# Keys and queries stored with the high and low part of a feature side by side, so that a head's tile is loaded on all 128 partitions

## The chip, the cores and the metric

One core of one Trainium2 chip runs the whole program. The metric is device time in microseconds (us). The kernel before took 2184.16 us, the median of three runs (2183.7 to 2186.5).

The core has TensorE (PE in the profile, with PEld for its weight loads), VectorE (DVE), ScalarE (ACT), GpSimd (POOL) and SyncE (SP). In this kernel nearly all DMA transfers are issued from SP's queue, in the order in which they stand there, and are carried out by 16 DMA engines that the profile shows as one busy share.

## The reference

One layer of a streaming encoder on 1024 positions of 1024 features, all in float32:

```
x = x + 0.5 * swiglu_ffn(rms_norm(x), ffn1)
u = rms_norm(x);  q_a k_a v_a q_b k_b v_b gate = split(u @ w_mix_in)
y_a = softmax(q_a k_a^T / 8 + rel_bias, band of 9 chunks of 64) v_a        # 8 heads of 64
p1, p2 = softmax(q_b[r] k_b[r]^T / 8 + t5_bias, chunk-causal)  r = 0, 1    # 4 heads, 2 x 64 features
y_b = rms_norm((p1 - lam * p2) v_b) * (1 - lambda_init)
x = x + (sig(g_a) * (y_a @ w_branch_a) + sig(g_b) * (y_b @ w_branch_b)) @ w_o
x = x + 0.5 * swiglu_ffn(rms_norm(x), ffn2);   out = rms_norm(x)
```

What matters here is the score product q k^T: 64 features per head, 1024 keys.

## The kernel before

**Split operands.** Large products are done three times: an operand is split into a part `hi`, which ScalarE rounds to float32r, and the rest `lo` (VectorE, source minus `hi`), and a product a·b becomes hi·hi + hi·lo + lo·hi (`mm3`, L128 to L130). The feed-forward and projection products are moreover done with a Strassen scheme of seven products on half matrices.

**The stages.** First feed-forward block (up to about 690 us of the profiled execution), the mixer's input projection (to about 1075 us), attention (1075 to about 1385 us), the output projection of the mixer, the second feed-forward block.

**Projection.** For each of eight index values n, `Pair` produces 128 features of the queries and 128 of the keys (n = 0 to 3: two heads of branch A each; n = 4 to 7: one head of branch B, whose two halves r are 64 features each), on [128 features, 512 positions] pieces. `qk_sink(n)` splits such a piece and writes `hi` and `lo` by `move` (L124) to the DRAM tensors `q_d[n]` and `k_d[n]`. Their shape is [2, 128, 1024]: all `hi` rows, then all `lo` rows. A piece is 256 KB, and a key piece costs two stores. The split pieces `qkh` lie in a ring of ten buffers (tag "f") that other pieces of the projection share.

**Attention.** For each n, `load_qkv(n)` brings three tiles of [128, 2, 1024] into SBUF (the middle index is the head, or r): `qs` holds `hi` of the 64 query features on partitions 0 to 63 and `lo` on 64 to 127; `ks` holds `hi` of the keys twice, `kl` holds `lo` twice. One matmul against `ks` (L775) and one against `kl` (L776) over 128 partitions then add up the four products. Since one DMA fills one half of the partitions, each n needs six DMAs of 512 KB ([64, 2, 1024]), then `vt` (values, 1 MB) and, for the A pairs and every second B head, eight DMAs of the bias `nb`.

The work of one n is a list of jobs (`jobs_a`: 8, `jobs_b`: 8 with growing width). `run` keeps up to four jobs in flight, a stage apart: scores and softmax (L775, L776, L783, L785), transposes `pt` (L791), the product with the values `pv` (L860 for A, L939 and L940 for B), and for B the output transpose `try` (L954). Between B's jobs `branch_a` puts pieces of the next projection, `pb` (12 matmuls each, L128 to L130), which load a gate piece `gl` and store the result (`ta`, L889).

**What sets the order.** The order of each engine's instructions is set when the program is built, by a scheduler that plays a model of the timeline; each engine then goes through its own list strictly in order and waits at an instruction whose operands are not there. SP does the same: an issue waits until its tile's buffer is free, and until the eighth DMA before it in the queue has landed (eight completion counters are used in turn). The tiles `qs`, `ks`, `kl`, `vt`, `y` and `nb` share a ring of 14 buffers (tag "big"), so that the loads of the next n are issued while the present one is worked on.

Of the kernel before, what the change touches and what calls it, by code (L numbers as in the profile page):

```python
# [10 lines left out]
F32R = mybir.dt.float32r  # L11
# [5 lines left out]
P = 128  # L17
S = 1024
# [3 lines left out]
HALF = 512  # L22
# [32 lines left out]
def hybrid_layer_kernel(ctx, tc, x, ffn1_norm, ffn1_w_in, ffn1_w_out, mix_norm, w_mix_in,  # L55
# [3 lines left out]
    nc = tc.nc  # L59
# [9 lines left out]
    def big(shape, name, dtype=F32R):  # L69
        return sb.tile(shape, dtype, tag="big", bufs=14, name=name)  # L70
# [7 lines left out]
    def temp(shape, name="temp"):  # L78
        return sb.tile(shape, F32, tag="f", bufs=TF, name=name)
# [14 lines left out]
    def split(src, hi, lo, scale=None, on_pool=False):  # L94

        if scale is None:
            nc.scalar.copy(out=hi, in_=src)  # L97
        else:
            nc.scalar.activation(out=hi, in_=src, func=AF.Copy, scale=scale)
        h = hi.bitcast(F32)  # L100
        if scale is None:
            (nc.gpsimd if on_pool else nc.vector).tensor_tensor(out=lo, in0=src, in1=h, op=ALU.subtract)  # L102
        else:
            nc.vector.scalar_tensor_tensor(out=lo, in0=src, scalar=scale, in1=h,
                                           op0=ALU.mult, op1=ALU.subtract)
# [16 lines left out]
    def move(eng, dst, src):  # L122

        eng.dma_start(out=dst.bitcast(F32), in_=src.bitcast(F32))  # L124
# [394 lines left out]
    def drams(n, shape, name, dtype=F32):  # L519
        return [dram.tile(shape, dtype, name=f"{name}{i}") for i in range(n)]  # L520
# [44 lines left out]
    x_part = drams(NT, [P, D], "xp")  # L565
    x_mid = drams(NT, [P, D], "xm")
    x_mix = drams(NT, [P, D], "xx")
    q_d = drams(8, [2, P, S], "q", F32R)
    k_d = drams(8, [2, P, S], "k", F32R)
    v_d = drams(2, [S, 2 * HALF], "v", F32R)  # L570
    g_d = drams(2 * KT, [P, S], "g")
    ta_d = drams(KT, [P, S], "ta")
# [65 lines left out]
    with tc.tile_pool(name="ps1", bufs=1, space=PSUM) as ps:  # L638
# [64 lines left out]
        def qk_sink(n):  # L703
            def sink(th, blk, ap):

                hi = sb.tile([P, HALF], F32R, tag="f", bufs=TF, name="qkh")
                own = (th, blk) != (1, 0)
                lo = ap if own else temp([P, HALF], "qkl")
                split(ap, hi, lo, scale=-0.125 if blk == 0 else None)
                lo = lo.bitcast(F32R)  # L710
                for c, v in enumerate((hi, lo)):
                    move(nc.sync, (k_d if blk else q_d)[n][c, :, th * HALF:(th + 1) * HALF], v)
            return sink

        def gate_sink(j):
# [31 lines left out]
    with tc.tile_pool(name="ps2", bufs=1, space=PSUM) as ps:  # L747
# [3 lines left out]
        nc.vector.tensor_tensor(out=e2, in0=e2, in1=e1, op=ALU.subtract)  # L751
        nc.vector.tensor_scalar(out=neg_lam, in0=e2, scalar1=-LAMBDA_INIT, scalar2=None, op0=ALU.add)

        def load_qkv(n):

            qs, ks, kl = (big([P, 2, S], name) for name in ("qs", "ks", "kl"))
            for c in range(2):
                half = slice(64 * c, 64 * c + 64)
                move(nc.sync, qs[half], q_d[n][c].rearrange("(h p) s -> p h s", p=64))
                for v, kt in enumerate((ks, kl)):  # L760
                    move(nc.sync, kt[half], k_d[n][v].rearrange("(h p) s -> p h s", p=64))
            vt = big([P, NT, 256], "vt")
            move(nc.sync, vt, v_d[n // 4].rearrange("(t p) c -> p t c", p=P)[:, :, (n % 4) * 256:(n % 4 + 1) * 256])
            return qs, ks, kl, vt
# [50 lines left out]
        def jobs_a(pr):  # L815
            ctx_ = {}

            def job(sb_, h):
                if not ctx_:
                    ctx_["qkv"] = load_qkv(pr)  # L820
                    ctx_["y"] = big([P, 2, S], "y")
                    ys.append(ctx_["y"])
                    ctx_["nb"] = big([P, 2, S], "nb", F32)
                    for hh in range(2):
                        bias_rows(ctx_["nb"][:, hh, :WA], diag_a, 2 * pr + hh, EA, WA)
# [67 lines left out]
        def jobs_b(hb, filler):  # L893
            ctx_ = {}

            def job(i):
                if not ctx_:
                    ctx_["qkv"] = load_qkv(4 + hb)
                    ctx_["y"] = big([P, 2, S], "y")
                    ys.append(ctx_["y"])  # L900
                    if hb % 2 == 0:
                        nbs.append(big([P, 2, S], "nb", F32))
                        for hh in range(2):
                            bias_rows(nbs[-1][:, hh, :], diag_b, hb + hh, EB, WB)
                    ctx_["nb"] = nbs[-1][:, hb % 2, :]
# [65 lines left out]
    with tc.tile_pool(name="ps3", bufs=1, space=PSUM) as ps:  # L971
# [3 lines left out]
        for jj in range(KT // 2):  # L975
            wr = load(w_cols(w_branch_b[0], jj * 256, 256, 0, 4), raw_tile([P, 4, 256]))
            for odd in range(2):
                j = 2 * jj + odd
                w = split_units(wr[:, :, odd * P:(odd + 1) * P], branch_unit)
                for th in range(2):  # L980
                    c = slice(th * HALF, (th + 1) * HALF)
# [80 lines left out]
```

## Time and profile before

| what | value |
|---|---|
| median of the runs | 2184.16 us |
| the profiled execution, its own time | 2184.25 us |
| its span, first to last instruction | 2181.9 us |
| PE busy | 2084.9 us (96%) |
| DVE busy | 1461.3 us (67%) |
| ACT busy | 977.4 us (45%) |
| SP queue's DMA (q1) | 319.55 MB, 47.9% of the 16 engines' span |
| mean granted TensorE clock | 0.985 |

The profiled execution's own time is 2.35 us more than its span, and 0.09 us above the median, so a microsecond of the span is taken as a microsecond of the time.

How to read it: "idle before, releaser" is the time for which an engine stood still ahead of an instruction, and what let it go on. The chain of waits is followed back from the last instruction, so work on it is work that set the end. In the table of windows each engine's busy time stands with the number of instructions, then PEclk (the granted share of TensorE's clock), the busy share of the DMA engines and what they moved.

### The profile page before, as it was taken

To read this page: it belongs to the slowest core of one execution; us is meant where nothing else is said; L and a number is where in the kernel's file an instruction comes from. 1 tells how busy PE (TensorE), PEld (TensorE's weight loads), DVE (VectorE), ACT (ScalarE), POOL (GpSimd) and SP (SyncE) were. 2 spreads that over 40 slices of the span, in tenths; PEclk is the share of its full clock that TensorE was granted. 3 is DMA by queue.
4 is the path that set the end of the run, shared out by engine and by line. 5 is a ranking of instruction groups with operands and counts; after the bars stand their busy time and mean duration, and the time that the engine had idled before them with its cause. 6 is when DMAs were issued, how large, how long until landed. Compare 5 with 4: busy or idle time off the path is not lost.

```text
span 2181.9 us, 29018 instructions
## 1 busy us (share of the span) xinstructions
PE 2084.9 (96%) x10025; PEld 1739.5 (80%) x10025; DVE 1461.3 (67%) x2678; ACT 977.4 (45%) x1911; POOL 195.6 (9%) x290
## 2 busy tenths in 40 slices
PE   6999999999999999999999878898999999999997
PEld 5788888888888788998788767676778888888886
DVE  7666565576578656556588767677766665658566
ACT  5433333334456444444588555235533333334444
POOL 2120000000000000000175233201000000000001
PEclk9999999999999999999999988999999999999999
DMA  6653233293354544443895675714543333366334
GB/s 191 175 167 113 91 107 102 91 373 105 116 167 128 164 136 164 135 151 125 210 210 122 156 180 157 243 64 145 173 130 120 96 114 97 116 221 233 98 116 158
DMA packets 273347, 325.16 MB, mean 149 GB/s; under 512 B 15292, under 2 KB 167884, under 8 KB 273200
## 3 DMA queue, kind: packets, MB, share of 16 engines
q1 hardware_dynamic: 271872, 319.55, 47.9%
q0 software_dynamic: 1184, 3.24, 0.6%
q8 instruction: 79, 1.29, 0.3%
q14 instruction: 68, 0.56, 0.1%
q10 hardware_dynamic: 144, 0.52, 0.1%
HBM read 226.45 MB, written 96.80 MB: 148 GB/s over the span
## 4 chain that ended last, share of the span: by engine, by line
PE 81%; DVE 7%; DMA 6%; ACT 3%; issue 2%; SPq 1%; POOL 0%; ACTq 0%; DVEq 0%; POOLq 0%
PE prod L128 18%; PE prod L129 18%; PE prod L130 18%; PE po L129 6%; PE po L130 6%; PE po L128 6%; DMA kl<-k 2%; DVE wlo L102 2%; PE tr L205 1%; ACT whi L97 1%; PE pt L791 1%; PE pb L128 1%; PE sc L775 1%; DMA ha<-hS 1%; PE pb L129 1%
## 5 line engine op out<-in xcount | busy, mean ns | idle before, releaser
L129 PE MATMUL po<-wlo,whi 128*128 128x512 f32 x728 | 284.7, 391 | 5.7 <-DVE wlo L102 5.5
L130 PE MATMUL po<-whi,wlo 128*128 128x512 f32 x728 | 283.4, 389 | 0.0
L97 ACT CAST whi<-raw 128x512 fp32r<-128x512 f32 x200 | 124.4, 622 | 308.6 <-PE prod L129 246.9
L97 ACT CAST whi<-T 128x512 fp32r<-128x512 f32 x196 | 121.9, 622 | 250.3 <-PE prod L129 225.1
L97 ACT CAST whi<-B 128x512 fp32r<-128x512 f32 x178 | 110.8, 623 | 266.0 <-PE po L129 258.0
L113 DVE TENSOR_TENSOR c<-prod,c 128x512 f32<-128x512 f32 x190 | 131.1, 690 | 134.6 <-PE prod L130 122.9
L102 DVE TENSOR_TENSOR wlo<-raw,whi 128x512 fp32r<-128x512 f32 x200 | 138.6, 693 | 105.1 <-ACT whi L97 66.4
L102 DVE TENSOR_TENSOR wlo<-B,whi 128x512 fp32r<-128x512 f32 x178 | 122.6, 689 | 126.7 <-ACT whi L97 126.6
L128 PE MATMUL po<-whi 128*128 128x512 f32 x728 | 198.4, 390 | 0.5 <-DVE xc L507 0.5
L102 DVE TENSOR_TENSOR wlo<-T,whi 128x512 fp32r<-128x512 f32 x196 | 134.7, 688 | 92.3 <-ACT whi L97 91.1
L139 POOL TENSOR_TENSOR r<-v,neg_half 128x1 f32<-128x1 f32 x64 | 53.8, 844 | 1326.8 <-DVE v L180 1227.1
L129 PEld LDWEIGHTS po<-wlo,whi 128*128 128x128 f32 x728 | 136.6, 188 | 37.7 <-DVE wlo L102 9.9
L128 PEld LDWEIGHTS po<-whi 128*128 128x128 f32 x728 | 136.2, 188 | 30.3 <-ACT whi L97 1.1
L130 PEld LDWEIGHTS po<-whi,wlo 128*128 128x128 f32 x728 | 136.7, 188 | 28.1
L102 DVE TENSOR_TENSOR wlo<-N,whi 128x512 fp32r<-128x512 f32 x64 | 44.1, 690 | 114.0 <-PE prod L129 62.8
L102 DVE TENSOR_TENSOR wlo<-ha,whi 128x512 fp32r<-128x512 f32 x154 | 105.7, 686 | 9.0 <-ACT whi L97 9.0
L272 ACT COPY c<-prod 128x512 f32<-128x512 f32 x186 | 103.1, 587 | 11.5 <-DMA hA<-c 4.0
L785 ACT ACTIVATE pm<-pm,mn 128x640 f32<-128x640 f32 (+7 forms) x128 | 94.1, 737 | 20.1 <-DVE mn L783 11.1
L783 DVE CUSTOM_DVE_ANT_0 pm<-sc,nb 128x640 f32<-128x640 f32 (+7 forms) x128 | 88.4, 699 | 21.5 <-PE sc L776 20.3
L97 ACT CAST whi<-ha 128x512 fp32r<-128x512 f32 x154 | 94.8, 615 | 16.9 <-PE prod L129 11.4
L128 PE MATMUL prod<-A11h,whi 128*128 128x512 f32 x240 | 96.0, 400 | 1.9 <-ACT A11h L97 1.9
L128 PE MATMUL prod<-S1h,whi 128*128 128x512 f32 x240 | 94.5, 394 | 2.4 <-ACT S1h L97 1.4
(246 smaller groups left out, 5398.3 us busy)
## 6 DMA issues: line engine op xcount, KB each, us to landing
raw<-in_ffn_w_in_dram SPq DMA_DIRECT2D x98, 512.0 KB, 4.4
raw<-in_w_mix_in_dram SPq DMA_DIRECT2D x47, 512.0 KB, 4.4
ha<-hS SPq DMA_DIRECT2D x88, 256.0 KB, 2.7
hA<-c SPq DMA_DIRECT2D x66, 256.0 KB, 4.3
ha<-hA SPq DMA_DIRECT2D x66, 256.0 KB, 2.7
B<-in_ffn_w_out_dram SPq DMA_DIRECT2D x12, 1024.0 KB, 10.6
hS<-hs SPq DMA_DIRECT2D x44, 256.0 KB, 2.8
hS<-c SPq DMA_DIRECT2D x44, 256.0 KB, 4.5
```

The costliest lines, as they stand in the source:

```text
L97: nc.scalar.copy(out=hi, in_=src)
L102: (nc.gpsimd if on_pool else nc.vector).tensor_tensor(out=lo, in0=src, in1=h, op=ALU.subtract)
L113: nc.vector.tensor_tensor(out=out_, in0=a, in1=b, op=op)
L128: nc.tensor.matmul(ps, a[0], b[0], start=first, stop=False, skip_group_check=shared)
L129: nc.tensor.matmul(ps, a[0], b[1], start=False, stop=False, skip_group_check=shared)
L130: nc.tensor.matmul(ps, a[1], b[0], start=False, stop=last, skip_group_check=shared)
L139: nc.gpsimd.tensor_tensor(out=r, in0=v, in1=neg_half, op=ALU.pow)
L205: nc.tensor.transpose(tr[:, k, :], rows[:, k * P:(k + 1) * P], ident)
L272: nc.scalar.copy(out=self.held[name], in_=p)
L775: nc.tensor.matmul(sc[:, m, :wc], qs[:, h, c], ks[:, h, kc], start=True, stop=False)
L783: nc.vector.tensor_tensor_reduce(out=d3, in0=sc, in1=nb.rearrange("p (n w) -> p n w", n=n), scale=1.0, scalar=3e38, op0=ALU.add, op1=ALU.m ...
L785: nc.scalar.activation(out=dst, in_=dst, func=AF.Exp, bias=mn, scale=-1.0, accum_out=rs)
```

## The change

`q_d` and `k_d` get the shape [128, 2, 1024]: for each feature a row `hi` and a row `lo`, one after the other. A third set of tensors `kx_d` holds the keys with the two rows the other way round (`lo`, `hi`). `qk_sink` writes each of the two parts of a key piece twice, once into `k_d` and once into `kx_d`.

`load_qkv` now reads, for each of the three tiles, 256 consecutive rows of 4 KB: rows 0 to 127 (features 0 to 63, both parts) for the first head or half, rows 128 to 255 for the second. Partition 2f holds `hi` of feature f and partition 2f + 1 its `lo`. `qs` against `ks` gives hi·hi + lo·lo, `qs` against `kl`, which is now read from `kx_d`, hi·lo + lo·hi: the same four products. A new argument `parts` could cut a load in pieces; every call leaves it at 1. Each n then needs three DMAs of 1 MB on 128 partitions in place of six of 512 KB on 64.

```diff
-    q_d = drams(8, [2, P, S], "q", F32R)
-    k_d = drams(8, [2, P, S], "k", F32R)
+
+    q_d = drams(8, [P, 2, S], "q", F32R)
+    k_d = drams(8, [P, 2, S], "k", F32R)
+    kx_d = drams(8, [P, 2, S], "kx", F32R)
...
                 for c, v in enumerate((hi, lo)):
-                    move(nc.sync, (k_d if blk else q_d)[n][c, :, th * HALF:(th + 1) * HALF], v)
+                    for d, dst in enumerate((k_d, kx_d) if blk else (q_d,)):
+                        move(nc.sync, dst[n][:, c ^ d, th * HALF:(th + 1) * HALF], v)
...
-        def load_qkv(n):
+        def load_qkv(n, parts=1):
+
 
             qs, ks, kl = (big([P, 2, S], name) for name in ("qs", "ks", "kl"))
-            for c in range(2):
-                half = slice(64 * c, 64 * c + 64)
-                move(nc.sync, qs[half], q_d[n][c].rearrange("(h p) s -> p h s", p=64))
-                for v, kt in enumerate((ks, kl)):
-                    move(nc.sync, kt[half], k_d[n][v].rearrange("(h p) s -> p h s", p=64))
+            for p in range(parts):
+                c = slice(p * S // parts, (p + 1) * S // parts)
+                for dst, src in ((qs, q_d[n]), (ks, k_d[n]), (kl, kx_d[n])):
+                    move(nc.sync, dst[:, :, c],
+                         bass.AP(src.tensor, src.offset + c.start, [[S, P], [P * S, 2], [1, S // parts]]))
```

The built program's order shows where this moves instructions. Up to the attention stage, the order on PE, DVE and ACT is as before, and SP's list differs by the 32 added stores, each right behind its twin. In the attention stage the scheduler's order differs on all engines, and at a few places behind it. Lines from `load_qkv` on lie three or four further down in the changed file (L775 becomes L779, L791 becomes L795, L939 becomes L943, L954 becomes L958, L889 becomes L893).

On SP, the loads for n = 5 (the second B head; `wa` is a weight of branch A, `gl` a gate piece, `ta` a result piece), before:

```order
L119 DMA wa<-in_w_branch_a_dram 128x4x256
L124 DMA qs<-q_180 64x2x1024
L119 DMA gl<-g_193 128x512
L124 DMA ks<-k_188 64x2x1024
L124 DMA kl<-k_188 64x2x1024
L124 DMA qs<-q_180 64x2x1024
L124 DMA ks<-k_188 64x2x1024
L124 DMA kl<-k_188 64x2x1024
L124 DMA vt<-v_192 128x8x256
```

And in the changed program:

```order
L119 DMA gl<-g_201 128x512
L119 DMA wa<-in_w_branch_a_dram 128x4x256
L124 DMA qs<-q_180 128x2x1024
L124 DMA ks<-k_188 128x2x1024
L124 DMA kl<-kx_196 128x2x1024
L124 DMA vt<-v_200 128x8x256
L893 DMA ta_217<-gl 128x512
```

Six loads have become three, the gate piece goes ahead of the weight, and the loads still stand behind that weight.

On PE, the first scores of n = 5 (`sc` of width 128, two for `ks` and two for `kl`), before:

```order
L939 MATMUL pv<-vt,whi 128x256
L940 MATMUL pv<-vt,wlo 128x128
L954 MATMUL try<-dg,o_11641 128x128
L775 MATMUL sc<-ks,qs 128x128 x2
L939 MATMUL pv<-vt,whi 128x256
L791 MATMUL pt<-ident,pm 128x128 x4
L940 MATMUL pv<-vt,wlo 128x128
L776 MATMUL sc<-kl,qs 128x128 x2
```

And in the changed program:

```order
L944 MATMUL pv<-vt,wlo 128x128
L779 MATMUL sc<-ks,qs 128x128
L795 MATMUL pt<-ident,pm 128x128
L779 MATMUL sc<-ks,qs 128x128
L780 MATMUL sc<-kl,qs 128x128 x2
L943 MATMUL pv<-vt,whi 128x256
L958 MATMUL try<-dg,o_11666 128x128
L944 MATMUL pv<-vt,wlo 128x128
```

The new head's scores now stand ahead of a `try` and of some `pv` of the old head that stood ahead of them before.

## Prediction

> **What bounds the kernel now.** I read the page first (its chain of waits), then PE's waits in the attention stage, then PE's timeline where it waits for a load, then the table of windows for the DMA engines, and last SP's timeline for when the loads were issued.
>
> The chain by engine and by line:
>
> ```profile
> PE 81%; DVE 7%; DMA 6%; ACT 3%; issue 2%; SPq 1%; POOL 0%; ACTq 0%; DVEq 0%; POOLq 0%
> PE prod L128 18%; PE prod L129 18%; PE prod L130 18%; PE po L129 6%; PE po L130 6%; PE po L128 6%; DMA kl<-k 2%; DVE wlo L102 2%; PE tr L205 1%; ACT whi L97 1%; PE pt L791 1%; PE pb L128 1%; PE sc L775 1%; DMA ha<-hS 1%; PE pb L129 1%
> ```
>
> TensorE sets the end nearly everywhere. The largest group that isn't an engine's is `kl<-k`, a load that this change rewrites. The chain in order of time, in the window of B's heads (start, us, what), shows it three times:
>
> ```profile
> 1203.82 16.16 DMA kl<-k
> ...
> 1252.32 13.16 DMA kl<-k
> ...
> 1298.17 16.73 DMA kl<-k
> ```
>
> These are the loads for n = 5, 6 and 7. What they cost is not their 46.05 us, since PE has old work for part of that, but what PE stood still. PE's waits from 1190 to 1340 us (total, times, longest), and the six rows of its timeline (start, duration; idle before in brackets):
>
> ```profile
> PE sc L775 <- DMA ks<-k: 16.9, 3, 8.0
> PE sc L776 <- DMA kl<-k: 3.0, 3, 1.6
> PE pb L128 <- DVE gl L888: 2.7, 1, 2.7
> ```
>
> ```profile
> 1212.55 0.44 PE L954 MATMUL try<-dg,o 128*128 128x128 f32 x2
> 1217.97 0.66 PE L775 MATMUL sc<-ks,qs 128*128 128x128 f32 x2 [4.99 <-DMA ks<-k]
> 1220.12 0.66 PE L776 MATMUL sc<-kl,qs 128*128 128x128 f32 x2 [0.21 <-DMA kl<-k]
> ...
> 1263.37 0.66 PE L775 MATMUL sc<-ks,qs 128*128 128x128 f32 x2 [3.91 <-DMA ks<-k]
> 1265.62 0.66 PE L776 MATMUL sc<-kl,qs 128*128 128x128 f32 x2 [1.14 <-DMA kl<-k]
> ...
> 1309.32 0.66 PE L775 MATMUL sc<-ks,qs 128*128 128x128 f32 x2 [8.04 <-DMA ks<-k]
> 1315.04 0.66 PE L776 MATMUL sc<-kl,qs 128*128 128x128 f32 x2 [1.64 <-DMA kl<-k]
> ```
>
> So PE stood 5.20, 5.05 and 9.68 us, 19.9 us in all, at the first scores of three heads. The other five n lose nothing there: their loads run under the work of the n before.
>
> A second cost follows each stall. The windows right behind them (us, then busy time and count of each engine, PEclk, DMA share, GB/s):
>
> ```profile
> 1217.20:1223.90 6.70, 5.72 (x26) 5.46 (x27) 3.30 (x17) 3.48 (x12) 1.40 (x3) 0.50 1.00 293
> 1261.60:1271.70 10.10, 7.12 (x29) 6.28 (x30) 3.38 (x8) 2.33 (x6) 2.38 (x3) 0.50 1.06 241
> 1305.90:1319.50 13.60, 8.53 (x37) 8.14 (x38) 2.65 (x11) 2.62 (x9) 0.45 (x1) 0.50 0.83 189
> ```
>
> After each stall TensorE's clock is granted at 0.50. The 5.72 + 7.12 + 8.53 = 21.4 us of matmuls in them would be 10.7 us at full clock. DVE and ACT are busy under half of these windows, so PE could use the time.
>
> **How fast a load could be.** A window while half tiles load, and two in which 128-partition transfers fill the DMA engines: the rows of `w_o` (2 KB) and the 4 KB rows of `xt` beside some stores.
>
> ```profile
> 1210.00:1220.00 10.00, 4.92 (x27) 4.30 (x25) 4.38 (x12) 1.93 (x5) 1.66 (x2) 0.86 1.04 215
> 1400.00:1410.00 10.00, 9.80 (x43) 7.58 (x41) 8.33 (x12) 1.87 (x3) 2.73 (x2) 1.00 1.04 387
> 2143.00:2148.00 5.00, 5.00 (x23) 4.13 (x22) 2.09 (x5) 2.95 (x6) 0.00 (x0) 1.00 1.02 290
> ```
>
> With the engines equally full, the half tiles move 215 GB/s (241 and 189 in the windows above), full ones 290 to 387. Both halves are in flight together and the rate is still the low one, so the halves don't add up. [...]
>
> **The change part by part.** *Six loads become three.* The bytes are the same, 3.15 MB (3 x 2^20 bytes) for each n. What matters is when they land for n = 5, 6, 7. SP's timeline gives the issues (start, duration, what):
>
> ```profile
> 1198.71 0.39 SPq L119 DMA_DIRECT2D wa<-in_w_branch_a_dram  x1
> ...
> 1245.83 0.59 SPq L124 DMA_DIRECT2D qs<-q  x1
> ...
> 1251.33 0.33 SPq L889 DMA_DIRECT2D ta<-gl  x1
> ...
> 1293.40 0.38 SPq L119 DMA_DIRECT2D wa<-in_w_branch_a_dram  x1
> ```
>
> For n = 5, 0.79 MB (`wa`, `gl`) and 3.15 MB go out from 1198.7. At 215 GB/s that is 18.3 us; `kl` in fact landed at 1219.98, 21.3 us after, so 3 us come on top for latency and for `vt`, which shares the engines. At 387 GB/s the same sum is 10.2 + 3 = 13.2 us: `kl` at 1211.9, `ks` a third of the load earlier at 1209.2. PE came to its first new score at 1212.99 (12.55 + 0.44). No stall is left. The changed order on PE brings that score forward by a `try` and one or two `pv`, about 1 us, which still fits.
>
> For n = 6, the second half of the loads stood behind a store `ta` that waited to 1251.33; three loads in a row no longer do. 3.15 + 0.26 MB from 1245.8 at 387 GB/s is 8.8 + 3 us, so `kl` lands at 1257.6; PE was free at 1259.46 (1263.37 less 3.91). No stall. For n = 7, 3.94 MB from 1293.4 land at 1306.6 (`ks` at 1303.9); PE was free at 1301.28. A stall of 2.6 us is left at `ks`, and I allow 4 us in all. So 19.9 - 4 = 15.9 us of standing still go.
>
> At the lower row, 290 GB/s, the three land at 1215.3, 1260.6 and 1310.0: stalls of about 2, 1 and 7 us stay, and 9.9 us go. At the other end all 19.9 go.
>
> *The clock.* With no stall at n = 5 and 6, their halved windows go: (5.72 + 7.12) / 2 = 6.4 us. Of the third I take half, 2.1 us, since a short stall is left: 8.5 us. Ends: 4 us (three short stalls each still drop the clock for part of the window) and 10.7. [...]
>
> [...]
>
> *Can the stage use it?* If PE were not what the rest of B waits for, the gain would only move. A window between two stalls, and the two halves of the stage:
>
> ```profile
> 1272.00:1301.00 29.00, 28.75 (x174) 25.40 (x174) 25.43 (x86) 19.17 (x54) 8.36 (x17) 1.00 0.47 137
> 1076.00:1190.00 114.00, 105.09 (x740) 91.86 (x740) 98.99 (x318) 100.44 (x261) 74.04 (x93) 1.00 0.84 188
> 1190.00:1385.00 195.00, 158.34 (x887) 138.66 (x886) 133.32 (x406) 102.26 (x271) 56.34 (x100) 0.89 0.62 164
> ```
>
> Between the stalls PE hardly pauses. In all of B it has 158.3 of 195 us; 24 us shorter, DVE's 133.3 would be 78%, so nothing else is in the way. In A, PE, DVE and ACT each are busy for 87 to 92%, and PE names no load among its waits. There the DMA engines are 0.84 full with half tiles, but the work runs ahead of them but for one wait, `nb` on DVE. I take 0.6 us for A. Ends: 4.5 us gained (half of PE's 8.9 idle us), 3 lost (a changed order on four starts, at some 0.75 us each, near the longest of PE's waits for `mn`).
>
> ```profile
> DVE pm L783 <- DMA nb<-diag_a: 0.6, 1, 0.6
> ```
>
> *32 more stores of 256 KB* in the projection. They are 8.4 MB, some 22 us of full DMA engines at 387 GB/s, and SP spends 0.32 us on each. What hides them: over the projection the DMA engines are 0.40 busy and PE never stands.
>
> ```profile
> 860.00:1047.00 187.00, 187.00 (x1143) 168.49 (x1142) 112.67 (x189) 80.17 (x152) 0.00 (x0) 1.00 0.40 140
> L124 SPq DMA_DIRECT2D k<-qkh x13: 319/320/420, 861.6 to 1056.3; - x13
> k<-qkh SPq DMA_DIRECT2D x16, 256.0 KB, 2.1
> ```
>
> Queued behind a second store on SP are the next weight loads, which have ten buffers to run ahead in, and the piece's own buffer is held some 0.7 us longer. I take 0. If the ring of ten buffers had no slack, each of the 16 key pieces could hold PE up for a landing, 2.1 us: 34 us. The first loads (n = 0) come behind these stores, and at the full rate they need less time than before: 0.
>
> *Fewer issues:* 24 SP issues of 0.6 us go, 32 of 0.32 come, off PE's path both.
>
> Sum: 15.9 + 8.5 + 0.6 - 0 = 25.0 us. 2184.25 - 25.0 = 2159.2; the median stands 0.09 below the profiled execution, so I forecast **2159 us**.
>
> **The rivals.**
>
> 1. *Everything goes.* No stall, no halved clock, and A's starts profit too: 19.9 + 10.7 + 4.5 = 35, so 2149 us. For it: A's engines are full of half tiles. Against: n = 7 has 7.9 us between its first issue and the free PE, less than the load needs. Chance 0.17.
> 2. *Half of it.* The tiles land at 290 GB/s and the short stalls still drop the clock, 9.9 + 4 = 13.9: 2170 us. For it: 290 is the only row with 4 KB rows from DRAM on 128 partitions. Against: stores and smaller packets are in that window too. Chance 0.18.
> 3. *Nothing.* The low rate belongs to the layout in DRAM or to seven loads at once and not to the 64 partitions; PE stands as before: 2184 us. Against it: the `xt` row is 4 KB wide too and faster. Chance 0.05.
> 4. *Slower.* The second stores hold the buffers of the projection. The place is the ring "f", the price 2.1 us for each of 16 key pieces, 34 us, less the 25 gained: 2193 us. It decides from 1.6 us for each piece. Against it: PE's waits there are nil and the engines 0.40 full. Chance 0.05.
>
> **How the numbers follow.** My forecast has 0.55. The range takes in rivals 1 and 2 with the bounds of A's order: 2148 to 2174. Faster by over 0.2% (4.4 us, about what a measurement of this kernel can tell from no change): the forecast, rivals 1 and 2, 0.90; within 0.2%: rival 3 and a little of 4, 0.06; slower 0.04.
>
> **What would show it.** In the changed profile: windows at n = 5, 6, 7 with a full DMA share and 290 to 390 GB/s in place of 215 (else rival 3); no wait of PE for `ks` at n = 5 and 6 and under 5 us at n = 7; PEclk at 1.00 through 1200 to 1300; the projection's windows with PE still at full and the DMA share up to about 0.5 (else rival 4); B's part of the span some 24 us shorter and A's as long as before. I am wrong if the loads are faster but PE waits as long for something else at the same scores, or if the issue of the loads itself slides back with the new order on SP.

## The result, and the profile after

| kernel | median | lowest to highest |
|---|---|---|
| before | 2183.93 us (4 runs) | 2180.88 to 2186.5 |
| after | 2157.08 us (4 runs) | 2155.78 to 2163.77 |

The ratio is 0.9884, with a 95% interval of 0.986 to 0.9908: 26.9 us less. The profiled execution of the changed kernel took 2157.48 us with a span of 2155.1 us, 26.8 us under that of the kernel before on both counts.

First the whole attention stage, from its first score to the start of its last `try`, as one row of the table of windows (us, then busy time and count of PE, PEld, DVE, ACT, POOL, then PEclk, DMA share, GB/s). Before:

```profile
1075.75:1376.75 301.00, 256.27 (x1599) 224.89 (x1600) 230.05 (x719) 201.44 (x528) 130.38 (x193) 0.94 0.70 172
```

After:

```profile
1076.94:1354.11 277.17, 247.37 (x1600) 216.67 (x1600) 230.08 (x719) 199.70 (x528) 129.84 (x193) 0.99 0.55 185
```

The stage is 23.8 us shorter. PE stood still for 301.00 - 256.27 = 44.7 us of it and now stands for 29.8: 14.9 us are idle time that went. The other 8.9 us are busy time: the same matmuls (1599 and 1600 in the rows) took less, with PEclk at 0.99 in place of 0.94. DVE does the same work in both (230.05 and 230.08 us).

PE's waits in the changed kernel, 1190 to 1340 us (total, times, longest), and the rows of its timeline at the first scores of n = 5, 6 and 7, with what stands ahead of them:

```profile
PE sc L779 <- DMA ks<-k: 2.2, 1, 2.2
PE pb L128 <- DVE gl L892: 2.2, 2, 1.6
...
PE sc L780 <- DMA kl<-kx: 1.4, 1, 1.4
```

```profile
1207.90 0.27 PE L779 MATMUL sc<-ks,qs 128*128 128x128 f32 x1
...
1209.94 0.44 PE L780 MATMUL sc<-kl,qs 128*128 128x128 f32 x2 [1.41 <-DMA kl<-kx]
...
1246.72 0.41 PE L779 MATMUL sc<-ks,qs 128*128 128x128 f32 x2
...
1290.69 0.73 PE L795 MATMUL pt<-ident,pm 128*128 128x128 f32 x5
1293.59 0.41 PE L779 MATMUL sc<-ks,qs 128*128 128x128 f32 x2 [2.17 <-DMA ks<-k]
```

The three stalls of 5.20, 5.05 and 9.68 us have become 1.41, none and 2.17 us: 3.6 us in place of 19.9. The chain of waits in this stretch still passes through loads: for n = 5 and 7 those that the new head's scores need, for n = 6 the bias, and for less long than before (start, us, what):

```profile
1198.32 11.58 DMA kl<-kx
...
1247.07 9.47 DMA nb<-diag_b
...
1283.53 9.92 DMA ks<-k
```

Windows while these loads run, with the DMA engines as full as before:

```profile
1200.00:1210.00 10.00, 7.94 (x47) 6.84 (x47) 8.43 (x22) 7.79 (x17) 1.87 (x4) 1.00 1.03 392
1210.00:1220.00 10.00, 9.93 (x54) 9.00 (x55) 8.51 (x32) 4.16 (x15) 3.20 (x5) 0.83 0.35 125
1240.00:1250.00 10.00, 6.97 (x40) 5.29 (x39) 8.10 (x27) 8.45 (x21) 4.26 (x9) 0.93 1.00 384
```

Where 215 GB/s went over full engines before, 392 and 384 go now, and 10 us later the engines are 0.35 full. And the projection, with the 32 added stores:

```profile
860.00:1047.00 187.00, 187.00 (x1143) 168.49 (x1141) 112.56 (x189) 80.07 (x151) 0.00 (x0) 1.00 0.51 173
```

PE never stands there, as before; the DMA share rose from 0.40 to 0.51.

### The profile page after: what moved, and what is told of

Its sections match the earlier page's. It is cut to its first block, busy times and chain, and to the rows that moved or that the text cites. A ratio compares the mean times of both kernels' runs of the same rounds, so it can differ in the third digit from the quotient of the medians.

```text
span 2155.1 us, 29016 instructions
## 1 busy us (share of the span) xinstructions
PE 2074.9 (96%) x10025; PEld 1730.3 (80%) x10025; DVE 1460.8 (68%) x2678; ACT 975.0 (45%) x1911; POOL 193.3 (9%) x290
## 4 chain that ended last, share of the span: by engine, by line
PE 80%; DVE 7%; DMA 5%; ACT 4%; issue 3%; SPq 1%; POOL 0%; ACTq 0%; DVEq 0%; POOLq 0%
PE prod L128 19%; PE prod L129 19%; PE prod L130 18%; PE po L129 6%; PE po L130 6%; PE po L128 6%; DVE wlo L102 2%; ACT whi L97 1%; ACT pm L789 1%; PE tr L205 1%; PE pb L128 1%; PE pb L130 1%; PE pb L129 1%; PE pt L795 1%; PE sc L779 1%
## 5 line engine op out<-in xcount | busy, mean ns | idle before, releaser
L97 ACT CAST whi<-ha 128x512 fp32r<-128x512 f32 x154 | 94.8, 615 | 16.9 <-PE prod L129 11.4
L789 ACT ACTIVATE pm<-pm,mn 128x640 f32<-128x640 f32 (+7 forms) x128 | 94.0, 736 | 11.9 <-DVE ri L924 6.3
```

The lines of the kernel that those rows point to most:

```text
L789: nc.scalar.activation(out=dst, in_=dst, func=AF.Exp, bias=mn, scale=-1.0, accum_out=rs)
```

## The experiments

In all of them the reading that decides is the attention stage, because the stages around it scatter. It scatters itself: two profiles of the kernel before differ by 1.4 us in it, two of the changed one by 1.9. "Outside" is the span less the attention stage, from one profile each:

| kernel | loads n = 0 / 1 to 4 / 5 to 7 | attention, us | PE busy in it | outside, us | median | ratio (95%) |
|---|---|---|---|---|---|---|
| before | halves | 301.0 | 256.3 | 1880.9 | 2183.93 | 1 |
| before, again | halves | 302.4 | 256.8 | 1878.8 | 2183.47 (1 run) | |
| new layout, loads in halves | halves | 303.5 | 259.9 | 1880.9 | 2186.8 | 1.0005 (0.9994 to 1.0017) |
| second stores only | halves | 304.2 | 258.0 | 1879.0 | 2188.46 | 1.0014 (1.0004 to 1.0024) |
| after | full | 277.2 | 247.4 | 1878.0 | 2157.08 | 0.9884 (0.986 to 0.9908) |
| after, again | full | 279.1 | 251.8 | 1875.4 | 2157.04 | 0.9869 (0.9851 to 0.9887) |
| six full loads | full | 277.2 | 251.5 | 1877.8 | 2155.19 | 0.9858 (0.9841 to 0.9875) |
| even and odd partitions | every second partition | 281.4 | 250.8 | 1878.7 | 2162.58 | 0.9894 (0.9879 to 0.9909) |
| full from n = 5 | halves / halves / full | 275.8 | 250.4 | 1882.5 | 2159.41 | 0.9874 (0.9852 to 0.9896) |
| full at n = 0 and from 5 | full / halves / full | 273.8 | 251.7 | 1879.3 | 2154.68 | 0.9865 (0.9846 to 0.9885) |
| B's loads in two pieces | full | 283.5 | 252.3 | 1878.9 | 2163.75 | 0.9897 (0.9879 to 0.9915) |

The theory that they test is the prediction's: the gain is that of transfers which reach all partitions at once. Against it stand three others: the layout in DRAM, the smaller number of DMAs, and the changed order of the work, which comes with either.

**1. The new layout, loaded in halves.** Layout, `kx` and second stores as in the change; each tile comes in two DMAs of 64 partitions again.

```diff
-            for p in range(parts):
+            for c in range(2):
...
-                    move(nc.sync, dst[:, :, c],
-                         bass.AP(src.tensor, src.offset + c.start, [[S, P], [P * S, 2], [1, S // parts]]))
+                    move(nc.sync, dst[64 * c:64 * c + 64],
+                         bass.AP(src.tensor, src.offset + 64 * c * S, [[S, 64], [P * S, 2], [1, S]]))
```

> The changed kernel's DRAM layout, second key store and results, but each tile is loaded in two DMAs of 512 KB, onto partitions 0 to 63 and then 64 to 127: rows of 4 KB, contiguous in DRAM as in the change. The order on PE is that of the kernel before. Theory (the 64 partitions set the rate): the loads run at about 215 GB/s again, PE waits some 19.9 us for ks and kl at n = 5, 6, 7, 2184 us (2180 to 2188). Rival (the DRAM layout sets the rate): loads at 390 GB/s and 2157 to 2162 us.

Measured: 2186.8 us, ratio 1.0005. No gain at all. PE waits 14.7 us for these loads from 1190 to 1340 us (19.9 before, and 19.9 expected) and 4.5 for `gl` (2.7 before); in the whole stage it stands still for 43.6 us against 44.7. The loads for n = 5 to 7 are as slow as before (operation, count, KB each, median us from issue to landing; in the kernel before 9.2, 10.6 and 13.6):

```profile
PE sc L778 <- DMA ks<-k: 12.2, 3, 6.6
PE pb L128 <- DVE gl L891: 4.5, 2, 3.0
PE sc L779 <- DMA kl<-kx: 2.5, 3, 1.3
```

```profile
qs<-q SPq DMA_DIRECT2D x6, 512.0 KB, 8.4
ks<-k SPq DMA_DIRECT2D x6, 512.0 KB, 10.5
kl<-kx SPq DMA_DIRECT2D x6, 512.0 KB, 12.8
```

It follows that the layout in DRAM alone is worth nothing.

**2. Six loads, each on 128 partitions.** As the changed kernel, but each tile in two DMAs of 512 KB, one per head (or half r), both on all 128 partitions.

```diff
-            for p in range(parts):
+            for h in range(2):
...
-                    move(nc.sync, dst[:, :, c],
-                         bass.AP(src.tensor, src.offset + c.start, [[S, P], [P * S, 2], [1, S // parts]]))
+                    move(nc.sync, dst[:, h],
+                         bass.AP(src.tensor, src.offset + h * P * S, [[S, P], [1, S]]))
```

> The changed kernel with six loads of 512 KB for each n, each on all 128 partitions (one head or half at a time). Theory (partitions set the rate): loads at about 390 GB/s, 2157 to 2163 us. Rival (the number of DMAs, with the eighth-DMA wait of SP's queue, set the pace): most of the gain is lost, 2175 to 2184 us.

Measured: 2155.19 us, ratio 0.9858. Same count and size of DMAs as in experiment 1, and the whole gain. The landings in the same stretch:

```profile
qs<-q SPq DMA_DIRECT2D x6, 512.0 KB, 5.5
ks<-k SPq DMA_DIRECT2D x6, 512.0 KB, 6.4
kl<-kx SPq DMA_DIRECT2D x6, 512.0 KB, 7.6
```

The number of DMAs isn't the cause. The scheduler's order on PE is another one here than in experiment 1; the next experiment keeps it fixed.

**3. Two DMAs of 64 partitions each, on the even and on the odd partitions.** The DRAM layout and the arrangement in SBUF are those of the change, but `hi` and `lo` are loaded apart: each DMA still fills only 64 partitions, every second one. `kl` comes from `k_d` with the rows exchanged, so that `kx_d` and its stores are gone. The cut shows `load_qkv` against the kernel before.

```diff
-                half = slice(64 * c, 64 * c + 64)
-                move(nc.sync, qs[half], q_d[n][c].rearrange("(h p) s -> p h s", p=64))
-                for v, kt in enumerate((ks, kl)):
-                    move(nc.sync, kt[half], k_d[n][v].rearrange("(h p) s -> p h s", p=64))
+                for dst, src, d in ((qs, q_d[n], c), (ks, k_d[n], c), (kl, k_d[n], 1 - c)):
+                    move(nc.sync, dst[c::2],
+                         bass.AP(src.tensor, src.offset + d * S, [[2 * S, 64], [P * S, 2], [1, S]]))
```

> Each tile is loaded in two DMAs of 64 partitions, the even ones and the odd ones, from the changed layout of q and k; the second key store is gone, as the low part goes to the even partitions of kl. Six loads of 512 KB, order on PE that of the kernel before. If what counts is how far the partitions reach over the memory and not their number: loads near 390 GB/s and 2157 to 2165 us with the old order on PE, the difference to the changed kernel being the order's share. If 64 partitions are slow wherever they lie: about 215 GB/s and 2184 us. [...]

Measured: 2162.58 us, ratio 0.9894. Landings for n = 5 to 7, and a window while such loads run; ahead of it the same for experiment 1:

```profile
1205.00:1215.00 10.00, 6.84 (x36) 5.47 (x35) 7.15 (x21) 6.54 (x17) 3.39 (x6) 0.87 1.06 232
```

```profile
qs<-q SPq DMA_DIRECT2D x6, 512.0 KB, 6.7
...
ks<-k SPq DMA_DIRECT2D x6, 512.0 KB, 7.2
kl<-k SPq DMA_DIRECT2D x6, 512.0 KB, 8.2
```

```profile
1203.00:1213.00 10.00, 8.41 (x51) 6.81 (x49) 8.96 (x23) 6.20 (x15) 3.90 (x7) 1.00 0.95 357
```

This sharpens the theory. 64 partitions in a row make a slow load here (232 GB/s), 64 that lie two apart a fast one (357): not how many partitions a DMA fills counts, but which.

The landings say how. For n = 5 all six loads are issued before the first of them lands, in both kernels, but they land one after another in the order of their issue. The last four 512 KB loads land at 1217.03, 1219.68, 1222.24 and 1224.57 us in experiment 1, about 2.5 us apart, which is 0.52 MB / 2.5 us = 210 GB/s, and at 1209.16, 1210.45, 1211.73 and 1213.04 us here, 1.3 us apart, which is 403. A 4 KB packet takes 322 ns in the one window and 159 in the other (medians; 329 in the kernel before from 1210 to 1220 us, 159 in the changed one from 1200 to 1210). This looks like loads that are carried out in turn and not side by side, so that two halves don't add up. Issuing a lower and an upper half by turns doesn't help either: for n = 4 of experiment 5 they land 2.5 us apart as well.

Two transfers that each fill 64 partitions, spread over the whole range, came near one that fills all 128 (357 against 392 GB/s). Why a block of 64 is the slow one is not shown by any run here.

This kernel has the order of the kernel before on PE, row for row. So the order is not what brings the gain: with the old one attention is 281.4 us long, 19.6 us shorter than before. The changed kernel has 277.2 and 279.1 in its two profiles, so its order, its three loads and its added stores together are worth 2 to 4 us on top, little more than the scatter; no run tells these apart.

**4. The second stores alone.** The kernel before, with each key piece stored a second time into a tensor that nobody reads.

```diff
+    kx_d = drams(8, [2, P, S], "kx", F32R)
...
-                    move(nc.sync, (k_d if blk else q_d)[n][c, :, th * HALF:(th + 1) * HALF], v)
+                    for dst in ((k_d, kx_d) if blk else (q_d,)):
+                        move(nc.sync, dst[n][c, :, th * HALF:(th + 1) * HALF], v)
```

> The kernel before with the 32 second key stores added to a tensor that nothing reads; loads as before. Theory (stores are hidden): 2184 us, within 2 us of the kernel before, and PE as full through the projection. Rival (the stores hold buffers, up to 2.1 us for each of 16 key pieces): up to 34 us slower, 2218 us.

Measured: 2188.46 us, 2.8 us over the median of the kernel before on that chip (2185.67), ratio 1.0014. The stores cost nothing in the projection, as said, but they cost at the point where it ends. Behind the last of them on SP stand loads of n = 0 and of the bias `nb`. VectorE's wait for `nb` at A's start (total, times, longest) with the second stores alone, its rows at the same two `pm` in the kernel before, and two windows with the second stores:

```profile
DVE pm L785 <- DMA nb<-diag_a: 7.8, 2, 6.3
```

```profile
1076.42 0.29 DVE L783 CUSTOM_DVE_ANT_0 pm<-sc,nb 128x128 f32<-128x128 f32 x1 [4.53 <-PE sc L776]
...
1077.76 0.29 DVE L783 CUSTOM_DVE_ANT_0 pm<-sc,nb 128x128 f32<-128x128 f32 x1 [0.69 <-PE sc L776]
```

```profile
1076.00:1080.00 4.00, 1.14 (x7) 0.68 (x5) 0.64 (x4) 1.80 (x5) 0.00 (x0) 1.00 0.66 204
1080.00:1084.00 4.00, 3.54 (x12) 2.97 (x13) 2.86 (x15) 2.35 (x8) 2.02 (x5) 0.57 1.01 301
```

VectorE stands still at these two `pm` in the kernel before too, for 5.22 us, put down to PE's scores. So what the late `nb` adds is not 7.8 us but 7.8 - 5.2 = 2.6, close to the 2.8 us of the time. PE was busy for 3.21 and 4.00 us in these two windows before, with PEclk at 1.00. SP's timelines show what is late: the two loads of `kl` for n = 0 are issued from 1063.73 us here, behind key stores that go out 1.6 to 3 us apart, and from 1057.39 in the kernel before; the second fence is the latter.

```profile
1057.63 0.32 SPq L124 DMA_DIRECT2D kx<-qkh  x1
1060.13 0.32 SPq L124 DMA_DIRECT2D k<-c  x1
1063.08 0.32 SPq L124 DMA_DIRECT2D kx<-c  x1
1063.73 1.24 SPq L124 DMA_DIRECT2D kl<-k  x2
```

```profile
1057.39 1.24 SPq L124 DMA_DIRECT2D kl<-k  x2
```

SP's own waits from 1054 to 1066 us, with the second stores alone, say for what these stores stood: for the half tiles `qs` and `ks` of n = 0, which stand eight places ahead of them in the queue.

```profile
SPq L124 <- DMA ks<-k: 3.9, 2, 2.6
SPq L124 <- DMA qs<-q: 2.1, 1, 2.1
```

In the changed kernel, where these are full tiles, `kl` goes out at 1060.76 us, the last of the eight `nb` of n = 0 lands at 1076.66, ahead of the first score at 1076.94, and VectorE's idle time ahead of the two `pm` is 4.84 us:

```profile
1060.76 0.62 SPq L124 DMA_DIRECT2D kl<-kx  x1
```

Experiment 1 has second stores and half tiles too, and the same late `nb` (7.6 us), but its time is only 1.1 us above the kernel before, which the interval doesn't tell from nothing.

**5 and 6. Which loads count.** Experiment 5 is the changed kernel with halves for n = 0 to 4 and full loads for n = 5 to 7; experiment 6 makes n = 0 full as well (`n >= 5 or n == 0` in both lines of the diff).

```diff
-            for p in range(parts):
-                c = slice(p * S // parts, (p + 1) * S // parts)
-                for dst, src in ((qs, q_d[n]), (ks, k_d[n]), (kl, kx_d[n])):
-                    move(nc.sync, dst[:, :, c],
-                         bass.AP(src.tensor, src.offset + c.start, [[S, P], [P * S, 2], [1, S // parts]]))
+            for dst, src in ((qs, q_d[n]), (ks, k_d[n]), (kl, kx_d[n])):
+                for c in range(1 if n >= 5 else 2):
+                    r = P if n >= 5 else 64
+                    move(nc.sync, dst[r * c:r * c + r],
+                         bass.AP(src.tensor, src.offset + r * c * S, [[S, r], [P * S, 2], [1, S]]))
```

> New layout and second key stores throughout, but only n = 5, 6, 7 load on all 128 partitions; n = 0 to 4 load the two halves of 64 partitions. If the gain is that of the three stalls and of the clock behind them, B takes 164 to 166 us (183.6 before, 164.4 in the changed kernel), A 117 to 120 us (117.4 before, 120.0 with half tiles and the second stores), and the time is 2165 to 2168 us, some 18 to 20 us under the kernel before. If A's 4.7 us come from the loads, A is then 5 to 7 us longer than the 112.8 of the changed kernel; if they come from something else (the order of the work in A, chance), A stays near 113 and the time at 2160 or below. Against both: if B's gain needs full loads ahead of n = 5 (through the DMA engines that they leave free), B stays above 172.

> As the kernel whose loads are full from n = 5 on, with n = 0 on all 128 partitions as well; only n = 1 to 4 load halves of 64. PE's order in A is the same as with n = 0 in halves, so A shows the loads alone. If the longer A of the half-tile kernels with second stores (119 to 120 us) is the late start alone (VectorE waits 7.8 us for nb behind n = 0's slow loads, and the clock falls at 1080 us), A falls to 111 to 114, the wait for nb goes below 1 us, and the time to 2152 to 2157, at or below the changed kernel. If the half tiles of n = 1 to 3 cost A something on their own, A stays at 116 or more and the time at 2159.

Measured for 5: 2159.41 us, ratio 0.9874; for 6: 2154.68 us, ratio 0.9865. The attention stage of each:

```profile
1077.20:1352.95 275.75, 250.39 (x1599) 218.36 (x1600) 230.24 (x719) 201.70 (x528) 131.04 (x193) 0.98 0.66 188
```

```profile
1077.02:1350.84 273.82, 251.74 (x1600) 219.33 (x1600) 230.36 (x719) 201.55 (x528) 131.09 (x193) 0.97 0.66 183
```

Three of the eight n bring the whole gain of the stage: with halves for the other five it is as short as in the changed kernel (275.8 against 277.2 and 279.1), and the time is 2.4 us longer than the changed kernel's on the same chip, with intervals that overlap. The order on PE in experiments 5 and 6 is a third one, neither that of the kernel before nor that of the changed kernel, so their stages can be compared with each other more closely than with either. The row also shows that A's and B's share can't be told apart by the first `pv` of B. By that mark A takes 117.4 us before, 112.8 after, 119.2 in experiment 5 and 116.3 in 6, but B then takes 183.6, 164.4, 156.6 and 157.5: what A gains B loses, since the order lets the heads overlap more or less. My expectation that B alone would be 164 to 166 us and the time 2165 to 2168 was read off that mark and missed by some 6 us.

Between 5 and 6 the order in A is the same on PE, and the start is what moves. VectorE's idle time ahead of the first two `pm` is 7.80 us in experiment 5, put down to `nb`, and 4.84 us in 6, put down to no DMA: 3.0 us less. PE has 2.55 us of work in the window from 1080 to 1084 us in the one, 4.00 in the other:

```profile
1080.00:1084.00 4.00, 2.55 (x10) 1.86 (x10) 1.67 (x12) 1.97 (x9) 1.48 (x4) 0.69 1.04 343
```

```profile
1080.00:1084.00 4.00, 4.00 (x19) 3.32 (x18) 2.83 (x12) 3.11 (x11) 2.16 (x5) 0.67 1.05 231
```

So the late start behind half tiles is real. What it costs is less clear: 1.9 us of the stage, as much as two profiles of one program differ, and in the times 4.7 us with ratios whose intervals overlap. The clock fell in both (0.69 and 0.67), so the late start can't be all that brings it down. I expected A at 111 to 114 us, which did not come (116.3), and the time at 2152 to 2157 us, which did.

**7. B's loads in two pieces.** The first 512 positions of all three tiles, then the others. All else as changed.

```diff
-                    ctx_["qkv"] = load_qkv(4 + hb)
+                    ctx_["qkv"] = load_qkv(4 + hb, 2)
```

> The changed kernel, with the loads of the four B heads cut in two by position: all three tiles' columns 0 to 511 first, then 512 to 1023, so that the first narrow scores (128 to 512 wide) need half of the bytes. PE's remaining waits on these loads in the changed kernel are 2.2 us (ks) and 1.4 us (kl), and two windows of 3.4 us at half clock cost 3.4 us more at the most: if those are what is left, the time falls by 3 to 7 us, to 2150 to 2154. If what is left is PE's own work and the wait of pb on gl (1.6 us), or if six issues on SP in place of three push the first piece back, it stays at 2157, within 3 us.

Measured: 2163.75 us, ratio 0.9897: no faster, and 6.7 us above the changed kernel on the same chip. PE's waits on these loads are 3.1 us in all against 3.6 in the changed kernel, though the first `ks` needs half of the bytes:

```profile
1291.29 0.41 PE L779 MATMUL sc<-ks,qs 128*128 128x128 f32 x2 [2.26 <-DMA ks<-k]
1292.55 0.69 PE L780 MATMUL sc<-kl,qs 128*128 128x128 f32 x2 [0.86 <-DMA kl<-kx]
```

The data came 2.3 us earlier at n = 7 (1291.29 against 1293.59), but the order asks for it 2.4 us earlier too: PE was free at 1289.03 in place of 1291.42. The order is laid out by a model that knows of the smaller pieces; that this is why it asks earlier is not shown. The rest of the loss is spread over short waits of the new order. The largest difference among PE's waits from 1050 to 1400 us, in this kernel and then in the changed one:

```profile
PE pt L795 <- DVE wlo L102: 8.1, 17, 2.5
```

```profile
PE pt L795 <- DVE wlo L102: 5.6, 16, 0.8
```

I can't name one cause for it.

**8. Both kernels once more.**

> The kernel before, unchanged, profiled once more, for the stretch behind the attention (last product of w_o to the end), where the changed kernel is 5.3 us shorter (666.2 against 671.5) with hardly a change in its instructions. If that is chance (windows of half clock that come in one execution and not in another), this profile differs from the first by some us there, and has its half-clock windows elsewhere. If it belongs to the kernels, it shows 671 again.

> The changed kernel, unchanged, beside the two others on this chip. 2157 us again (2155 to 2160), B 163 to 166, A 112 to 115. The stretch behind the attention 666 if its 5.3 us belong to the kernel, 667 to 671 if they are chance. The six full loads by head (2155.2) are then the better kernel only if this stays 2 us or more above.

Measured: 2183.47 us for the one run of before, 2157.04 us for after. Attention is 302.4 and 279.1 us, 23.3 apart; the stretch from the last product of `w_o` to the end is 668.4 and 665.8 us, 2.6 apart and not 5.3. Rows for the first and the second profile of the kernel before, in that stretch:

```profile
1510.43:2181.91 671.48, 650.45 (x2870) 534.66 (x2868) 436.04 (x692) 269.79 (x480) 11.45 (x13) 0.98 0.43 140
```

```profile
1512.83:2181.24 668.41, 647.57 (x2870) 532.09 (x2868) 435.96 (x692) 269.80 (x480) 9.71 (x13) 0.99 0.43 140
```

The same program differs by 3.1 us with the same work, 2.9 of it in PE's busy time, with PEclk at 0.98 and 0.99. Over all eleven profiles, what lies outside the attention stage takes 1875.4 to 1882.5 us whatever the loads are. About 3 us of the 26.8 lie there, in both pairs of profiles; they are not above this scatter, and I don't explain them.

## Why the prediction was right

It said 2159 us, within 2148 to 2174, and 2157.08 was measured, which is 26.9 us of gain against 25.0. The forecast had the whole gain in the attention stage, where 23.8 us came (23.3 in the second pair of profiles); the other 3 us lie outside it, as said above, and were not forecast. That the totals agree within 2 us is partly luck.

*The bound.* PE's standing at the first scores of n = 5, 6 and 7 was the right place. Experiment 5 makes only these three loads full and has the stage as short as the changed kernel, though with another order on PE.

*The rate.* The sum took 387 GB/s: 392 and 384 were seen. By the rows' ratio of 387 to 215 the three loads of the chain would have come from 46.05 to 25.6 us, and they did not: the three `kl` took 11.58, 10.83 and 11.99 us from issue to landing, 34.4 in all (each now holds 1 MB and has `qs` and `ks` ahead of it). The sum did not use this figure. "Both halves are in flight together" holds for their issue only: they land one after another (experiment 3). For n = 5 the sum was 13.2 us from the first issue to `kl`; from the issue of `wa` it was 1198.32 + 11.58 - 1196.82 = 13.1, though `gl` had gone ahead of `wa` by then. For n = 6 the sum was 11.8 us from `qs` to `kl`, and 11.9 were measured. For n = 7 it was 10.5 us to `ks`; measured from the issue of `wa` it was 1283.53 + 9.92 - 1282.03 = 11.4.

```profile
1196.82 0.38 SPq L119 DMA_DIRECT2D wa<-in_w_branch_a_dram  x1
...
1282.03 0.38 SPq L119 DMA_DIRECT2D wa<-in_w_branch_a_dram  x1
```

The 3 us for latency and for what shares the engines, taken from one load before, held within about a microsecond for all three.

*The stalls.* Predicted: 15.9 of 19.9 us go, with 2.6 us left at `ks` of n = 7. Measured: 2.17 left there, and 1.41 at `kl` of n = 5, where none was expected; the 4 us allowed in all cover both. The load of n = 5 took as long as computed, but PE came 5 us earlier (first new score at 1207.90 against 1212.99) where the prediction allowed about 1. For n = 6 and 7 the prediction left the issues and the free PE where they stood, and both moved: for n = 6 the first issue came at 1237.24 in place of 1245.83 us and PE at 1246.72 in place of 1259.46. `ks` of n = 6 landed at 1246.58, 0.14 us ahead of its score, so "No stall" came true by little. At n = 7 the load took 0.9 us more than its sum and PE came free 9.4 us behind the first issue in place of 7.9: two misses that cancel, so that 2.17 stands so near to 2.6 is luck. All told 16.3 us of these stalls went, and 14.9 us of PE's idle time in the stage: the rest came back as short waits for DVE, ACT and POOL. In the second pair of profiles it is 18.3 us of idle time (302.4 - 256.8 against 279.1 - 251.8).

*The clock.* Predicted 8.5 us. Measured as PE's busy time for the same matmuls: 8.9 in the first pair, 5.0 in the second. The size is right in the first pair and too large by 3.5 us in the second, and the places are not right: I expected 1.00 through 1200 to 1300 us and a short stall's loss at n = 7. The 2.17 us stall there cost no clock, but windows at half clock stand behind n = 5 and in n = 6 (PEclk 0.83 and 0.93 in the rows above). In the second profile of the changed kernel the stall of 1.21 us at n = 5 cost no clock (1.00 from 1210 to 1220 us), and from 1460 to 1490 us PEclk is 0.94 in the first profile and 1.00 in the second, so the places change from one execution to the next.

*A's starts.* The 0.6 us can't be confirmed as such. By the first `pv` of B, A is 4.6 us shorter and B 19.2, where the prediction had A as long as before and B some 24 shorter; as experiments 5 and 6 show, this mark doesn't tell the two apart. Full loads at n = 1 to 4 gave nothing that the profiles show (experiment 6 does without them); at n = 0 they keep the added stores from costing some 2 us (2.8 us of the time in experiment 4, 1.9 us of the stage between experiments 5 and 6).

*The stores.* "I take 0" was right for the changed kernel, and for the reason given in the projection, where PE's row is 187.00 of 187.00 us. But the zero hung on a cover that was named only as "at the full rate they need less time than before": with half tiles ahead of them in SP's queue the same stores cost 2.8 us (experiment 4; 1.1 in experiment 1, not clear of noise), at A's start and not in the ring "f". Rival 4 had the wrong place and a price more than ten times too large.

*The rivals.* Rival 3 (the layout, or the number of loads) fell with experiments 1 and 2. Rival 2 fell with the rate. Rival 1 wanted all stalls, all clock and half of A's idle time; no run reached its 2149 us.

The thing my words had wrong is the number of partitions. Rival 3 set the layout against "the 64 partitions", and experiment 3 shows that 64 partitions can load nearly at the full rate when they are spread over all 128.

## What to carry to other kernels

A load that fills the upper or the lower 64 partitions ran at about 0.55 of the rate that the same bytes get over all partitions (215 against 392 GB/s here), and issuing both halves at once did not help, since they landed one after the other; interleave the two operands by partition, so that each DMA spreads over the whole range, and the number of DMAs may stay as it is. Price such a change by the stalls of the engine that waits, counting from the load's first issue, and add the clock that TensorE loses behind them (worth 8.9 and 5.0 us in the two pairs of profiles here); speeding up the transfers that work hides already brought nothing here (full loads at n = 1 to 4: a stage of 277.2 us with them, and of 273.8 without them in experiment 6, with another order on PE). An added store is not free because the engines are idle (2.8 us in experiment 4): look at what stands behind it in its queue when the stage ends.

## What the runs showed of the hardware beside that

Half of the partitions is not half of the rate: every second partition gives 357 GB/s (experiment 3), a block of 64 gives 232 in the like window of experiment 1. The busy share of the DMA engines hides this: it is 0.95 and 1.06 in these windows, since each 4 KB packet of the slow loads takes twice as long (322 against 159 ns).

TensorE's half-clock stretches don't follow the longest stall. They begin on a grid: in the changed kernel at 1211.1, 1248.7 and 1354.5 us, which are 11 and 31 steps of 3.41 us apart. Windows of one step, the one ahead of a half-clock stretch and the stretch itself, then the one that holds most of the 2.17 us stall and the one behind it:

```profile
1207.70:1211.10 3.40, 1.99 (x17) 1.77 (x16) 2.01 (x12) 2.55 (x8) 0.46 (x1) 1.00 1.07 359
...
1211.10:1214.50 3.40, 3.40 (x17) 3.40 (x17) 2.41 (x10) 1.42 (x7) 1.79 (x2) 0.50 0.25 94
```

```profile
1289.66:1293.07 3.41, 1.76 (x14) 1.44 (x13) 1.96 (x6) 2.71 (x8) 1.24 (x2) 1.00 1.02 420
1293.07:1296.48 3.41, 2.88 (x22) 2.56 (x22) 1.79 (x7) 1.06 (x3) 0.95 (x2) 1.00 1.05 370
```

PE was busy for 59% of the step that was followed by half clock, and for 52% of the one that was not. The first profile of the kernel before has such a grid too, at another place: its clock falls at 1217.1, 1261.5, 1305.9 and 1350.3 us, 13 steps apart each, and 1217.1 lies 1.76 steps behind 1211.1. In these two profiles I summed PE's busy time for each step at full clock from 1070 to 1378 us. All seven steps with 43% or less were followed by the lower clock, and none with 64% or more was; of those between, two with 59 and 61% were, and four with 46, 52, 58 and 60% were not. The idle time alone doesn't decide: 1.41 us of it in one step were followed by half clock, 1.65 in the other were not. What decides between 46 and 61% stays open.
